# First-stage vectors through PSUM, leading products by kinds, and a fixed order of state-space banks in a two-block network on one core

## The chip, the cores and the metric

One core of a Trainium2 chip runs the whole kernel. TensorE multiplies, VectorE, ScalarE and GpSimd work on tiles, SP and ScalarE issue transfers. The metric is device time in microseconds from one launch; less is better. The kernel before took 1715.83 us in the median of three runs (1713.58 to 1717.22).

## The reference

A 512 x 1024 activation `x` goes through two blocks in fp32. Cut to what matters:

```python
x = layer_norm(x, ln_emb_g, ln_emb_b)                  # first stage
h = x @ w_in + b_in                                    # q, k, v, indexer, latents
mix = concat([swa_sink_attention(...), dsa_attention(...)]) @ w_o + b_o
x = layer_norm(ALPHA * x + mix, ln1_g, ln1_b)          # first norm
ca = memory_cross_attention(x, mem, ...)               # keys of mem are needed here
x = layer_norm(ALPHA * x + ca, ln2_g, ln2_b)           # second norm
f = square(relu(x @ w_up + b_up)) @ w_down + b_down
x = layer_norm(ALPHA * x + f, ln3_g, ln3_b)            # third norm
u = rms_norm(x, norm_w[0]); x = x + ssd_mixer(u, ...)  # state space: z, xbc, dt from u
u = rms_norm(x, norm_w[1]); x = x + mla_mixer(u, ...)  # fourth norm before it
return rms_norm(x, final_norm_w)
```

## The kernel before

Every fp32 operand of a product is split into a high and a low part, and a product is three: high by high, high by low, low by high (`mm3`, lines 129 to 131; which of 130 and 131 holds the low activations depends on which operand is stationary). `wload` (lines 115 to 125) brings a 512 KB weight into one of three raw buffers on SP's queue, ScalarE makes the high half (line 121), GpSimd the low half in two pieces (line 124); five split buffers follow. Activations are split by ScalarE (line 145) and VectorE (line 146) out of a PSUM bank of four transposes (`xpose`, line 279). The token axis has four tiles of 128 (`NT`).

The code is written as dataflow; a framework lays out each engine's instructions in one fixed order beforehand (`TileContext(..., schedule_with_timeline_sim=True)`) and inserts the waits. At run time every engine and queue keeps that order. PSUM has eight banks; `banks(...)` closes the pool of banks and opens one with other names (`acc`, `mm`, `px` and so on), and a bank that had another use before is waited for tile by tile.

First stage (`block1`): keys of the memory (`mem_k`, eight weights `xa_wk`, 24 products of 256 columns each) run while four tiles of `x` arrive. Each tile gets statistics (lines 326, 327), an inverse root (`nrstd`, lines 102 to 106: one ScalarE root, then four VectorE instructions of one column), gain and bias (lines 329, 330), its transposes, and later `ALPHA * r + b_o` (line 334), stored to `hd`. Gain, bias and `b_o` are rows of 1024 that are brought as 128 copies. Then `win_m` (96 products of 328 columns, accumulators `acc`), then `win_s`.

At every norm a helper `gemm_lead` (lines 170 to 182) computes the first four tiles of the next product while the last tokens are still being normalised: for token half 0 to 255, then 256 to 511, for each of four weights, for eight slices, one `mm3`. Between them `flush` issues the deferred transposes of the later tokens. It serves `xa_wq` (first norm), `w_up` (second), `ssm_xbc` (third) and `mla_z` (fourth). At the third norm `gate0` (line 1182) computes the gate products `z` of two token tiles ahead of it; the other two run in the state-space stage in banks `px`.

State-space stage (`block2a`): `conv` (lines 946 to 951) reads the four leading tiles in their banks, `ssm_dt` and `ssm_cum` make the decays, `prep` and `core` the chunks. Its banks are named `mm`, `px`, `py`, `po`.

Of the kernel before, what the change touches and what calls it, by code (L numbers as in the profile page):

```python
# [12 lines left out]
P = 128  # L13
# [11 lines left out]
class Net:  # L25
    def __init__(self, ctx, tc, a):
# [7 lines left out]
        self.banks(acc=4, mm=4)  # L34
# [28 lines left out]
    def mm(self):  # L63
        return self.bank("mm")
# [33 lines left out]
    def nrstd(self, pool, v, n, eps):  # L98
# [6 lines left out]
        nc.vector.scalar_tensor_tensor(y1, y0, v, y0, op0=ALU.mult, op1=ALU.mult)  # L105
        nc.vector.scalar_tensor_tensor(v, y1, -3.0, y0, op0=ALU.add, op1=ALU.mult)
# [63 lines left out]
    def gemm_lead(self, aps, X, tags):  # L170
        XH, XL = X
        W = [self.wload(ap) for ap in aps]
        pss = [self.bank(tag) for tag in tags]
        for lo in (0, 256):
# [115 lines left out]
    def block1(self, dbg):  # L290
# [21 lines left out]
        g = self.nbcast(lnp, "ln_emb_g", D, eng=nc.sync)  # L312
        b = self.bcast(lnp, "ln_emb_b", D, eng=nc.sync)
# [35 lines left out]
        snk = self.bcast(ap, "swa_sinks", 8)  # L349
        iw = ap.tile([P, NT, 8], F32, name="iw")  # L350
        bs = self.load(ap, "bin_s", [P, 13])
# [14 lines left out]
        rows = self.rows_load(self.mp)  # L366
        bm = self.bcast(ap, "bin_m", 328)
        kvg = self.bcast(ap, "dsa_kv_norm_g", P)
        ikg = self.bcast(ap, "idx_k_ln_g", 64)
        ikb = self.bcast(ap, "idx_k_ln_b", 64)  # L370
# [4 lines left out]
        for c, nk in enumerate((3, 3, 2)):  # L375
            wh, wl = self.wload(a["win_m"][:, c * 984:c * 984 + nk * 328], n=nk * 328)
            for kk in range(nk):
# [4 lines left out]
                k += 1  # L382
        cf = ap.tile([P, NT, P], F32, name="cf")
# [1258 lines left out]
```

## Time and profile before

| what | value |
|---|---|
| median of three runs | 1715.83 us (1713.58 to 1717.22) |
| profiled run | 1716.78 us |
| its span, first to last instruction | 1714.8 us |
| mean granted TensorE clock | 0.990 |
| TensorE busy | 1657.8 us, 97% |
| VectorE, ScalarE, GpSimd busy | 913.5, 835.6, 889.2 us |

The profile is of one execution. TensorE's busy time counts overlapping products once. In the rows, PE is TensorE, PEld its loads of the stationary operand, DVE VectorE, ACT ScalarE, POOL GpSimd, SP SyncE; `ACTq` and `SPq` are what an engine's sequencer issues. Idle time of an engine is put down to the instruction that released it.

### The profile page before, as it was taken

The numbers are of one execution on the slowest core, as the hardware profiler recorded it, in microseconds if no ns is written. First come the engines' busy times: TensorE is split into PE (matmuls) and PEld (weight loads), VectorE is DVE, ScalarE is ACT, GpSimd is POOL, SyncE is SP. The second block draws the span as 40 slices with busy tenths as digits, with TensorE's granted clock in tenths as the row PEclk, the third lists the DMA queues.
The fourth block names the chain that finished last, engine by engine and source line by source line (L and its number), as shares of the span: only waits on it lengthen the run. The fifth ranks groups of instructions, "written<-read, shape, count | busy, mean of one in ns | idle before, by whom it ended". The sixth has DMA issues, their size and how long they took to land.

```text
span 1714.8 us, 27158 instructions
## 1 busy us (share of the span) xinstructions
PE 1657.8 (97%) x10203; PEld 1477.9 (86%) x10203; DVE 913.5 (53%) x1965; ACT 835.6 (49%) x1694; POOL 889.2 (52%) x817
## 2 busy tenths in 40 slices
PE   6999999999999999999899999999999999999998
PEld 6877888889988888888878898889999888988998
DVE  7579763743663004402769877779221307667512
ACT  4455664453353124412558777776333426565532
POOL 6756433363374445543556777776544544344431
PEclk9999999999999999999999999999999999999999
DMA  8634313332232222222433333332434442123341
GB/s 286 201 104 130 105 50 114 127 111 78 96 111 98 86 98 93 92 98 78 145 107 99 99 110 100 105 112 86 148 110 136 137 132 66 54 69 97 107 142 50
DMA packets 68178, 187.20 MB, mean 109 GB/s; under 512 B 9968, under 2 KB 16544, under 8 KB 67792
## 3 DMA queue, kind: packets, MB, share of 16 engines
q1 hardware_dynamic: 50128, 152.95, 27.4%
q10 hardware_dynamic: 17632, 30.43, 5.6%
q8 instruction: 80, 1.31, 0.3%
q0 software_dynamic: 288, 2.10, 0.3%
q14 instruction: 50, 0.41, 0.1%
HBM read 163.86 MB, written 14.78 MB: 104 GB/s over the span
## 4 chain that ended last, share of the span: by engine, by line
PE 80%; DVE 10%; issue 3%; ACT 3%; DMA 2%; POOL 1%; ACTq 0%; DVEq 0%; SPq 0%; POOLq 0%
PE mm L129 15%; PE mm L131 15%; PE mm L130 15%; PE acc L130 5%; PE acc L131 5%; PE acc L129 5%; PE sc L130 2%; PE sc L131 2%; PE sc L129 2%; PE pv L130 1%; PE pv L131 1%; PE pv L129 1%; PE tr L887 1%; POOL wl L124 1%; DVE sc L479 1%
## 5 line engine op out<-in xcount | busy, mean ns | idle before, releaser
L124 POOL TENSOR_TENSOR wl<-wraw,wh 128x512 fp32r<-128x512 f32 (+1 forms) x498 | 658.0, 1346 | 509.7 <-ACT wh L121 477.4
L121 ACT ACTIVATE wh<-wraw 128x1024 fp32r<-128x1024 f32 (+4 forms) x254 | 258.5, 1019 | 409.6 <-PE acc L131 123.7
L129 PE MATMUL mm<-xaH,wh 128*128 128x512 f32 x552 | 221.2, 401 | 3.2 <-DVE qbL L140 1.3
L130 PE MATMUL mm<-xaL,wh 128*128 128x512 f32 x552 | 220.4, 399 | 0.0
L131 PE MATMUL mm<-xaH,wl 128*128 128x512 f32 x552 | 220.0, 399 | 0.0
L129 PE MATMUL mm<-wh,xaH 128*128 128x256 f32 x512 | 147.2, 288 | 1.4 <-ACT xaH L145 1.4
L130 PE MATMUL mm<-wl,xaH 128*128 128x256 f32 x512 | 145.6, 284 | 0.0
L131 PE MATMUL mm<-wh,xaL 128*128 128x256 f32 x512 | 145.2, 284 | 0.0
L129 PEld LDWEIGHTS mm<-xaH,wh 128*128 128x128 f32 x552 | 104.4, 189 | 27.2 <-DVE qbL L140 1.8
L131 PEld LDWEIGHTS mm<-xaH,wl 128*128 128x128 f32 x552 | 104.4, 189 | 23.7
L130 PEld LDWEIGHTS mm<-xaL,wh 128*128 128x128 f32 x552 | 104.5, 189 | 23.0
L878 POOL TENSOR_SCALAR S<-S,den 128x128 f32<-128x128 f32 (+1 forms) x96 | 50.9, 534 | 105.1 <-DVE den L877 89.0
L129 PEld LDWEIGHTS mm<-wh,xaH 128*128 128x128 f32 x512 | 97.8, 191 | 2.0 <-ACT xaH L145 1.8
L130 PEld LDWEIGHTS mm<-wl,xaH 128*128 128x128 f32 x512 | 97.7, 191 | 0.2
L131 PEld LDWEIGHTS mm<-wh,xaL 128*128 128x128 f32 x512 | 97.0, 190 | 0.1
L129 PE MATMUL mm<-wh,xbH 128*128 128x256 f32 x336 | 94.9, 283 | 0.7 <-DVE lnsum L256 0.5
L131 PE MATMUL mm<-wh,xbL 128*128 128x256 f32 x336 | 94.4, 284 | 0.1
L130 PE MATMUL mm<-wl,xbH 128*128 128x256 f32 x336 | 94.3, 282 | 0.0
L698 DVE TENSOR_TENSOR rl<-rl 128x512 f32<-128x512 f32 x32 | 43.7, 1366 | 78.4 <-ACT rl L697 78.4
L948 DVE SCALAR_TENSOR_TENSOR xbc<-mm,conv_w,xbc 128x511 f32<-128x511 f32 (+2 forms) x84 | 62.2, 741 | 11.6 <-ACT xbc L946 10.9
L876 ACT ACTIVATE S<-S,mx 128x128 f32<-128x128 f32 (+1 forms) x96 | 53.7, 560 | 24.2 <-DVE mx L875 22.1
L129 PEld LDWEIGHTS mm<-wh,xbH 128*128 128x128 f32 x336 | 63.6, 189 | 1.6 <-DVE lnsum L256 0.7
(633 smaller groups left out, 4747.4 us busy)
## 6 DMA issues: line engine op xcount, KB each, us to landing
wraw<-in_w_up SPq DMA_DIRECT2D x32, 512.0 KB, 3.3
wraw<-in_w_down SPq DMA_DIRECT2D x32, 512.0 KB, 3.2
wraw<-in_ssm_xbc SPq DMA_DIRECT2D x32, 512.0 KB, 3.3
Dm<-acd ACTq DMA_DIRECT2D x32, 256.0 KB, 3.2
wraw<-in_ssm_out SPq DMA_DIRECT2D x16, 512.0 KB, 3.5
wraw<-in_mla_z SPq DMA_DIRECT2D x16, 512.0 KB, 3.5
wraw<-in_mla_out SPq DMA_DIRECT2D x16, 512.0 KB, 3.6
wraw<-in_ssm_z SPq DMA_DIRECT2D x14, 512.0 KB, 3.3
```

Source lines behind the costliest of these rows:

```text
L121: nc.scalar.activation(h[:, :n], raw[:, :n], AF.Copy)
L124: (leng or nc.gpsimd).tensor_tensor(l[:, e], raw[:, e], f32(h[:, e]), op=ALU.subtract)
L129: mm(out, aH, bH, start=first, stop=False, skip_group_check=True)
L130: mm(out, aH, bL, start=False, stop=False, skip_group_check=True)
L131: mm(out, aL, bH, start=False, stop=last, skip_group_check=True)
L479: nc.vector.match_replace(out=scs[n], in_to_replace=m8, in_values=scs[n], imm_value=-3e38)
L698: nc.vector.tensor_tensor(r, r, r, op=ALU.mult)
L876: nc.scalar.activation(s, s, AF.Exp, bias=mx, scale=-1.0, accum_out=den)
L878: nc.gpsimd.tensor_scalar(s, s, den, 1.0, op0=ALU.mult, op1=ALU.mult)
L887: self.nc.tensor.transpose(pt[:, c], S[:, c], self.ident)
L948: nc.vector.scalar_tensor_tensor(o[:, j:], ps[:, :T - j], cw[:, m, 3 - j:4 - j], o[:, j:], op0=ALU.mult, op1=ALU.add)
```

## The change

Five edits. (1) Gain, bias and `b_o` come as one row each; each row is split, and TensorE spreads it over 128 partitions by a product with a row of ones (minus ones for the gain), into `gb` banks; lines 329, 330 and 334 work on halves and read PSUM. The pool of the first stage is `acc=2, mm=2, gb=4` and is reopened as `acc=4, mm=4` after the additions of `b_o`. (2) Small loads (`xa_bk`, `swa_sinks`, `bin_s`, `bin_m`, gains, the rows of biases) go from ScalarE's queue to SP's; the rows and `xa_bv` are issued after `win_m`. (3) Lines 105 and 106 take their second tensor as a column scalar. (4) `gemm_lead` and `gate0` run by kinds: high by high for all tiles, then low weights, then low activations. (5) The state-space pool takes its banks in the order `mm`, `po`, `px`, `py`.

```diff
-        self.banks(acc=4, mm=4)
+        self.banks(acc=2, mm=2, gb=4)
@@ nrstd
-        nc.vector.scalar_tensor_tensor(y1, y0, v, y0, op0=ALU.mult, op1=ALU.mult)
-        nc.vector.scalar_tensor_tensor(v, y1, -3.0, y0, op0=ALU.add, op1=ALU.mult)
+        nc.vector.tensor_scalar(y1, y0, v, y0, op0=ALU.mult, op1=ALU.mult)
+        nc.vector.tensor_scalar(v, y1, -3.0, y0, op0=ALU.add, op1=ALU.mult)
@@ gemm_lead
+        def kind(x, ts, q, last=False):
+            for i in ts:
+                for k in range(8):
+                    c = slice(k * P, (k + 1) * P)
+                    mm(pss[i][:, q], W[i][x == 2][:, c], (XH, XL)[x == 1][:, k, q], start=x == 0 and k == 0, stop=last and k == 7, skip_group_check=True)
         for lo in (0, 256):
             q = slice(lo, lo + 256)
-            for (wh, wl), ps in zip(W, pss):
-                for k in range(8):
-                    c = slice(k * P, (k + 1) * P)
-                    self.mm3(ps[:, q], wh[:, c], wl[:, c], XH[:, k, q], XL[:, k, q], k == 0, k == 7)
-                self.flush(n=1)
+            kind(0, range(4), q)
+            self.flush(n=1)
+            kind(2, (0, 1), q)
+            self.flush(n=1)
+            kind(1, (0, 1), q, True)
+            kind(1, (2, 3), q)
+            self.flush(n=1)
+            kind(2, (2, 3), q, True)
             self.flush()
@@ block1
-        g = self.nbcast(lnp, "ln_emb_g", D, eng=nc.sync)
-        b = self.bcast(lnp, "ln_emb_b", D, eng=nc.sync)
+        gb = lnp.tile([1, 3, D], F32, name="gb")
+        for i, key in enumerate(("ln_emb_g", "ln_emb_b", "b_o")):
+            nc.sync.dma_start(gb[:, i, :], a[key].unsqueeze(0))
+        self.kb = self.load(self.mp, "xa_bk", [P, 8], eng=nc.sync)
+        gbs = self.pair(lnp, [1, 3, D], "gbs")
+        def spread(i, v):
+            sg = lnp.tile([1, P], F32R, name=self.nm("sg"))
+            nc.scalar.activation(sg, self.mhalf[0:1, 0:1].to_broadcast([1, P]), AF.Copy, scale=-2.0 * v)
+            self.split(gbs[0][:, i, :], gbs[1][:, i, :], gb[:, i, :])
+            B = [self.bank("gb") for _ in range(2)]
+            for h in range(2):
+                for x in range(2):
+                    nc.tensor.matmul(B[h], sg, gbs[x][:, i, h * 512:h * 512 + 512], start=x == 0, stop=x == 1)
+            return B
+        GB = spread(0, -1.0) + spread(1, 1.0)
...
-        self.kb = self.load(self.mp, "xa_bk", [P, 8])
         self.mem_k(W, wk)
-        bo = self.bcast(lnp, "b_o", D, eng=nc.sync)
-        self.vb = self.bcast(self.mp, "xa_bv", D, eng=nc.sync)
...
-            nc.vector.scalar_tensor_tensor(r, r, mv[:, 0:1], g, op0=ALU.subtract, op1=ALU.mult)
-            nc.vector.scalar_tensor_tensor(r, r, mv[:, 1:2], b, op0=ALU.mult, op1=ALU.add)
+            for h in range(2):
+                rh = r[:, h * 512:h * 512 + 512]
+                nc.vector.scalar_tensor_tensor(rh, rh, mv[:, 0:1], GB[h], op0=ALU.subtract, op1=ALU.mult)
+                nc.vector.scalar_tensor_tensor(rh, rh, mv[:, 1:2], GB[2 + h], op0=ALU.mult, op1=ALU.add)
             self.xpose(r, xt, t)
+        B = spread(2, 1.0)
         for t in range(NT):
-            nc.vector.scalar_tensor_tensor(r, r, ALPHA, bo, op0=ALU.mult, op1=ALU.add)
+            for h in range(2):
+                rh = r[:, h * 512:h * 512 + 512]
+                nc.vector.scalar_tensor_tensor(rh, rh, ALPHA, B[h], op0=ALU.mult, op1=ALU.add)
             nc.sync.dma_start(self.hd[t], r)
         lp.close()
+        self.banks(acc=4, mm=4)
...
-        snk = self.bcast(ap, "swa_sinks", 8)
+        snk = self.bcast(ap, "swa_sinks", 8, eng=nc.sync)
...
-        rows = self.rows_load(self.mp)
-        bm = self.bcast(ap, "bin_m", 328)
+        bm = self.bcast(ap, "bin_m", 328, eng=nc.sync)
...
+        rows = self.rows_load(self.mp)
+        self.vb = self.bcast(self.mp, "xa_bv", D, eng=nc.sync)
@@ block1b
-        self.zpre = [self.gate0(self.bank("z"), W, t) for t in range(2)]
+        self.zpre = [self.bank("z") for _ in range(2)]
+        for kinds in ((0, 2), (1,)):
+            for t in range(2):
+                self.gate0(self.zpre[t], W, t, kinds)
@@ block2a
-        self.banks(mm=3, px=2, py=2, po=1)
+        self.banks(mm=3, po=1, px=2, py=2)
+        for tag, n in self.tags.items():
+            for _ in range(n):
+                self.bank(tag)
@@ gate0
+        for x in kinds:
+            for k in range(8):
+                n = slice((k % 3) * 288, (k % 3) * 288 + 288)
+                self.nc.tensor.matmul(ps[:, :288], u[x == 1][:, k, q], W[k // 3][x == 2][:, n], start=x == 0 and k == 0, stop=x == 1 and k == 7, skip_group_check=True)
```

## Rows read from the trace of the kernel before

**Rows 1.** Page, busy time, share of the span and instructions of each engine.

```profile
PE 1657.8 (97%) x10203; PEld 1477.9 (86%) x10203; DVE 913.5 (53%) x1965; ACT 835.6 (49%) x1694; POOL 889.2 (52%) x817
```

**Rows 2.** Waits of TensorE, whole span: waiter, releaser, total us, times, longest.

```profile
PE acc L129 <- ACT wh L121: 9.0, 3, 7.9
PE mm L279 <- DVE res L330: 4.7, 2, 4.4
PE sc L130 <- DVE xbL L146: 4.0, 1, 4.0
...
PE sc L130 <- DVE lnmu L264: 2.7, 1, 2.7
```

**Rows 3.** Waits of TensorE from 810 to 865 us.

```profile
PE px L129 <- DVE dts L1199: 2.8, 1, 2.8
PE z L131 <- DVE lnmu L265: 1.2, 1, 1.2
PE z L131 <- DVE lnmu L264: 1.0, 1, 1.0
PE z L131 <- DVE xaL L146: 0.8, 1, 0.8
```

**Rows 4.** Stretches: length, busy of PE, PEld, DVE, ACT, POOL, clock, DMA, GB/s.

```profile
0.00:15.80 15.80, 7.26 (x30) 6.58 (x31) 6.30 (x14) 6.37 (x8) 7.19 (x12) 1.00 0.88 308
15.80:32.70 16.90, 10.58 (x78) 9.33 (x77) 16.90 (x24) 5.95 (x10) 11.69 (x8) 1.00 0.86 327
32.70:48.20 15.50, 15.46 (x119) 15.46 (x119) 12.13 (x15) 8.32 (x13) 13.91 (x9) 0.89 0.63 188
48.20:62.90 14.70, 14.70 (x100) 14.70 (x98) 6.04 (x9) 6.57 (x10) 14.04 (x12) 1.00 0.84 260
839.08:852.70 13.62, 13.62 (x118) 13.62 (x117) 8.36 (x16) 9.20 (x15) 5.23 (x6) 1.00 0.29 87
```

**Rows 5.** Timeline of VectorE at the first norm: start, us, instruction, [idle before].

```profile
316.54 0.14 DVE L103 TENSOR_SCALAR lnvar<-lnvar 128x1 f32<-128x1 f32 x1
...
317.99 1.10 DVE L105 SCALAR_TENSOR_TENSOR nr<-nr,lnvar 128x1 f32<-128x1 f32 x1
...
319.08 2.29 DVE L576 SCALAR_TENSOR_TENSOR res<-res,xa_bo 128x1024 f32<-128x1024 f32 x1
321.30 1.21 DVE L106 SCALAR_TENSOR_TENSOR lnvar<-nr 128x1 f32<-128x1 f32 x1
...
322.50 1.27 DVE L146 TENSOR_TENSOR xbL<-tr,xbH 128x512 fp32r<-128x512 f32 x2
```

**Rows 6.** Groups of VectorE up to 63 us: busy, mean ns | idle before.

```profile
L334 DVE SCALAR_TENSOR_TENSOR res<-res,b_o 128x1024 f32<-128x1024 f32 x4 | 7.9, 1986 | 3.3 <-PE mm L279 3.3
L330 DVE SCALAR_TENSOR_TENSOR res<-res,mv,ln_emb_b 128x1024 f32<-128x1024 f32 x4 | 7.1, 1781 | 0.0
L329 DVE SCALAR_TENSOR_TENSOR res<-res,mv,ln_emb_g 128x1024 f32<-128x1024 f32 x4 | 6.1, 1529 | 0.0
L146 DVE TENSOR_TENSOR xaL<-mm,xaH 128x512 fp32r<-128x512 f32 x8 | 5.2, 677 | 0.0
...
L105 DVE SCALAR_TENSOR_TENSOR nr<-nr,mv 128x1 f32<-128x1 f32 x4 | 3.6, 912 | 0.0
```

**Rows 7.** Timeline of VectorE, last instruction of the first stage.

```profile
51.66 1.28 DVE L146 TENSOR_TENSOR xaL<-mm,xaH 128x512 fp32r<-128x512 f32 x2
```

**Rows 8.** Timeline of ScalarE and its queue, first stage and first norm.

```profile
12.52 1.06 ACT L121 ACTIVATE wh<-wraw 128x1024 fp32r<-128x1024 f32 x1 [3.10 <-DMA ng_dsa<-in_ng_dsa]
...
59.26 0.33 ACTq L71 DMA_DIRECT2D swa_sinks<-in_swa_sinks  x1
...
323.76 1.04 ACT L121 ACTIVATE wh<-wraw 128x1024 fp32r<-128x1024 f32 x1
```

**Rows 9.** Line 1078, all of its instructions: ns least, median, longest.

```profile
L1078 DVE TENSOR_SCALAR gss<-gss x16: 157/170/1462, 920.6 to 1215.1; 128x2 f32<-128x2 f32 x16
```

**Rows 10.** Page, issues of transfers: KB each, median us to landing.

```profile
wraw<-in_w_up SPq DMA_DIRECT2D x32, 512.0 KB, 3.3
```

More of the change, by code (lines that the diff above doesn't have):

```diff
@@ L173, in gemm_lead @@
         pss = [self.bank(tag) for tag in tags]
+        mm = self.nc.tensor.matmul
+        def kind(x, ts, q, last=False):
[3 more added lines that the diff above has]
+                    mm(pss[i][:, q], W[i][x == 2][:, c], (XH, XL)[x == 1][:, k, q], start=x == 0 and k == 0, stop=last and k == 7, skip_group_check=True)
         for lo in (0, 256):
             q = slice(lo, lo + 256)
-            for (wh, wl), ps in zip(W, pss):
-                for k in range(8):
-                    c = slice(k * P, (k + 1) * P)
-                    self.mm3(ps[:, q], wh[:, c], wl[:, c], XH[:, k, q], XL[:, k, q], k == 0, k == 7)
-                self.flush(n=1)
+            kind(0, range(4), q)
[6 more added lines that the diff above has]
+            kind(2, (2, 3), q, True)
             self.flush()
@@ L348, in block1 @@
         masks = {n: ap.tile([P, (n + 1) * P], F32R, name=f"mk{n}") for n in range(1, NT)}
-        snk = self.bcast(ap, "swa_sinks", 8)
+        snk = self.bcast(ap, "swa_sinks", 8, eng=nc.sync)
         iw = ap.tile([P, NT, 8], F32, name="iw")
-        bs = self.load(ap, "bin_s", [P, 13])
+        bs = self.load(ap, "bin_s", [P, 13], eng=nc.sync)
         c2 = ctx.enter_context(ExitStack())
@@ L365, in block1 @@
         ap = c3.enter_context(self.pool("small"))
-        rows = self.rows_load(self.mp)
-        bm = self.bcast(ap, "bin_m", 328)
-        kvg = self.bcast(ap, "dsa_kv_norm_g", P)
-        ikg = self.bcast(ap, "idx_k_ln_g", 64)
-        ikb = self.bcast(ap, "idx_k_ln_b", 64)
+        bm = self.bcast(ap, "bin_m", 328, eng=nc.sync)
+        kvg = self.bcast(ap, "dsa_kv_norm_g", P, eng=nc.sync)
+        ikg = self.bcast(ap, "idx_k_ln_g", 64, eng=nc.sync)
+        ikb = self.bcast(ap, "idx_k_ln_b", 64, eng=nc.sync)
         ms = [ap.tile([P, 328], F32, tag="ms", name=self.nm("ms"), bufs=4) for _ in range(NT)]
@@ L828, in rows_load @@
     def rows_load(self, ap):
-        return (self.load(ap, "bk_swa", [32, 384]), self.load(ap, "bk_dsa", [32, 640]), self.load(ap, "ng_swa", [8, 384]),
-                self.load(ap, "ng_dsa", [8, 640]), self.load(ap, "rel_bias", [32, 16]))
+        return [self.load(ap, k, s, eng=self.nc.sync) for k, s in (("bk_swa", [32, 384]), ("bk_dsa", [32, 640]), ("ng_swa", [8, 384]), ("ng_dsa", [8, 640]), ("rel_bias", [32, 16]))]
     def bias_tile(self, bt, ud, h, n, w):
@@ L1180, in gate0_w, with gate0 @@
         return [self.wload(self.a["ssm_z0"][:, c * 864:c * 864 + nk * 288], n=nk * 288) for c, nk in enumerate((3, 3, 2))]
-    def gate0(self, ps, W, t):
+    def gate0(self, ps, W, t, kinds=(0, 2, 1)):
         u = self.u
         q = slice(t * P, (t + 1) * P)
-        for k in range(8):
-            wh, wl = W[k // 3]
-            n = slice((k % 3) * 288, (k % 3) * 288 + 288)
-            self.mm3(ps[:, :288], u[0][:, k, q], u[1][:, k, q], wh[:, n], wl[:, n], k == 0, k == 7)
+        for x in kinds:
+            for k in range(8):
+                n = slice((k % 3) * 288, (k % 3) * 288 + 288)
+                self.nc.tensor.matmul(ps[:, :288], u[x == 1][:, k, q], W[k // 3][x == 2][:, n], start=x == 0 and k == 0, stop=x == 1 and k == 7, skip_group_check=True)
         return ps
```

## The prediction

> **What bounds the kernel now.** First the busy shares: TensorE is busy for 97% of the span, every other engine for about half [rows 1]. So whatever is removed from another engine counts only where TensorE stands still for it, and the next view is who TensorE waits for [rows 2]. The reader is to see how short that list is: 9.0 us on the first weights (7.9 of them before anything has arrived), 4.7 us in the first stage on VectorE (line 330) and 4.0 and 2.7 us at two norms on the low halves of the transposed activations (`xbL`, and a count that VectorE reaches late). One stretch, from the third norm on, adds 1.2, 1.0 and 0.8 us in the gate products `z` and 2.8 us at a state-space bank `px` [rows 3]. The change touches all of these but the first 7.9 us.
>
> Third, the stretches [rows 4]. Where nothing is missing, 118 products, nearly all 256 columns wide, fill 13.62 us, so one costs 0.12 us, one of 512 columns about 0.24. Up to 15.8 us 30 products keep TensorE busy for 7.26 us, 0.24 each: the start runs at half pace. From 15.8 to 32.7 it works 10.58 of 16.90 us, while VectorE is busy in all 16.90. From 32.7 to 48.2 it is full, but at a granted clock of 0.89.
>
> Fourth, why VectorE is late. At the first norm an instruction of one column takes 0.14 us at line 103, and 1.10 and 1.21 at lines 105 and 106 a moment later; these two read two tensors from SBUF, line 103 one, and GpSimd computes low halves of weights meanwhile. The additions with two SBUF tensors stretch likewise: line 576 took 2.29 us [rows 5], line 334 1.99 in the mean, while reading one operand from PSUM costs 0.677 us for 512 columns eight times over [rows 6]. VectorE instructions with two SBUF tensors wait for GpSimd; those with one do not, if they are one column wide.
>
> **The change part by part.** Terms are against the span of 1714.8 us; the profiled run took 1716.78, 0.95 above the median of 1715.83. I subtract them from the median.
>
> *First stage.* Removed are three broadcasts of 512 KB (gain, bias, `b_o`), and a fourth (`xa_bv`) moves behind `win_m`; 2.1 MB at 308 to 327 GB/s is 6.5 us of transfer out of a saturated beginning [rows 4]. That counts only where data was last, about 1.1 us of the 9.0. GpSimd's sign change goes too (off the path). VectorE now: lines 329, 330 and 334 took 6.1, 7.1 and 7.9 us [rows 6], 21.1 together. After: 24 halves with a PSUM operand at 0.677, 16.2. Line 105 took 3.6 for four, at 0.14 it is 0.6. Added are three splits of a 1024-column row, priced by the whole 1024-column split that two halves of 0.677 make: 1.35 each, 4.1. Net VectorE: -4.9 -3.0 +4.1 = -3.8, and line 106 saves some 2 more by the same reasoning. TensorE adds 12 products of 512 columns: eight while it runs at half pace (0.48) and four later (0.24), 4.8 us. ScalarE adds three splits and three short rows, in stretches where it works 6 of 16 us [rows 4].
>
> TensorE's sum: it would reach `win_m` at 48.2 - 4.7 (the wait for line 330) - 1.7 (15.5 us at 0.89 rather than near 1) - 1.1 (weights) + 4.8 = 45.5. There the new wait lies: `win_m`'s four accumulators are the first banks that the reopened pool hands out; if a pool hands out banks by the order of first use, as the code reads, these are the four `gb` banks. Two of them are read by VectorE to the last of the eight additions of `b_o`. VectorE ended its stage at 51.66 + 1.28 = 52.9 [rows 7]; less 5.8 that is 47.1, and the additions now come last. Behind the waiting product stand the other `win_m` products on TensorE, and then everything. Two of the four token tiles can start earlier (the bias halves are free after the last norm), so I count half of the 1.6 us: `win_m` begins at 46.3, and the stage gains **1.9 us**. Bounds: a gain of 6.0, if the broadcast products fall into idle time and no bank is late; a loss of 4.7, if VectorE still ends at 52.9 and all 14.7 us of `win_m` [rows 4] follow it (67.6 for 62.9).
>
> The small loads leave ScalarE's queue: its split of the second weight sat 3.10 us behind them [rows 8]. TensorE waited little there, so I count nothing. They now stand in SP's queue, past the weight loads; a weight load issues only when a raw buffer comes free, so small loads fit between, and a few tenths of issue each are hidden by three raw and five split buffers. Without that cover see the slow rival.
>
> *Four instructions of each norm.* Lines 105 and 106 become instructions with one tensor and two column scalars. No row shows this form. The nearest is line 103, 0.14 us beside a busy GpSimd [rows 5]; the far end is line 1078, two columns, 157 to 1462 ns [rows 9]. I take 0.14, as the width is the same. Elsewhere than in the first stage this only makes VectorE earlier at the norms, and is counted with them.
>
> The Trainium skill's "SBUF — State Buffer" (section "Who interferes with whom") speaks against this edit: an instruction with a scalar instead of a second tensor may enter a mode that takes both ports of VectorE, and then either engine blocks the other for a whole instruction. "VectorE: DVE Perf Modes" (section "Mode 2×_2P") ties that to an even count, or an odd one that is equal for source and destination; one column is the latter. Line 1078 behaves as the rule says, line 103 does not [rows 5, 9]; by the rule the edit would bring nothing, and rival 2 is how that would come out.
>
> *First norm's leading products* (`xa_wq`). TensorE stops for 4.0 us because products with `xbL` come early, and `xbL` is made at 322.50, behind lines 105, 576 and 106 [rows 2, 5]. By kinds, 32 products need only the high halves and 16 more only the low halves of weights: 48 x 0.12 = 5.8 us of work that covers the 4.0. But the fourth weight's high half starts only at 323.76 [rows 8], and the first kind wants all four. It stands behind ScalarE's square, which waits for VectorE; without 0.96 us at line 105 and 1.07 at 106 it comes at about 321.7 and is there at 322.8. TensorE's lead began near 318.6 (the 4.0 us end with the first half of `xbL` near 323.1, and four products ran ahead), so 24 products have ended at 321.5. I take 4.0 - 1.2 = **2.8 us** (1.0 to 4.0).
>
> *Second norm* (`w_up`): 2.7 us in the same place [rows 2]; its four weights are earlier, so **2.4 us** (1.0 to 2.7).
>
> *Third norm* (`z`, then `ssm_xbc`). Three waits on low halves, 1.2, 1.0 and 0.8 us, stand in the gate products [rows 3]. By kinds 32 gate products come before any with low activations. I take **2.6 us** of the 3.0 (1.0 to 4.0, the upper end if the second tile also comes 1.0 us earlier by line 105, as at the first norm). The fourth norm's lead has no row among the longer waits: **0.3 us** (0 to 0.8).
>
> The price of the kinds: of the four tiles of a lead the first is ready 32 products, 3.8 us, later than before, and two 1.9 us. They are read by ScalarE and VectorE while TensorE computes the next tiles in other banks; that covers it. If it does not, the next stage's first tile waits up to 3.8 us.
>
> *State-space banks.* `px` was first used, so it took the first two banks, which the leading products still held until the convolutions had read them: a gate tile waited 2.8 us [rows 3]. With the order of banks fixed, `px` gets the two that served the transposes of the norm, free long before. The wait is put down to line 1199, the addition of `dt`'s bias, which stands in VectorE's queue right behind the convolutions, and it reads another tile's bank; so I hold the bank to be the cause. Late next is the chain from the convolutions to the decays; the tiles that it starts from now end some 2 us later against TensorE. No row prices that; its bounds are nothing and the whole 2.8, and I take 0.8 of loss, near the lower one, because the same chain also starts from the gate tile, which comes earlier now: **2.0 us** (0 to 2.8).
>
> Sum: 1.9 + 2.8 + 2.4 + 2.6 + 0.3 + 2.0 = 12.0; 1715.83 - 12.0 = **1703.8 us**.
>
> **The rivals.**
> 1. *Everything lands at its good end*, because a freed VectorE also frees ScalarE's queue, where splits of weights stand behind roots and squares that wait for VectorE (the split at 323.76 is one) [rows 8]. First stage 6.0, norms 3.6 + 2.7 + 3.8 + 0.5, banks 2.8: 19.4, so 1696.4.
> 2. *The edited norm still waits for GpSimd*, as line 1078 does [rows 9]. Then line 105 keeps its 3.0 us in the first stage and 106 its 2, the additions of `b_o` end later and `win_m` with them: a loss of 1.5 for the gain of 1.9, and each of three norms loses about 0.8: 12.0 - 3.4 - 2.4 = 6.2, so 1709.6. For it: the row of two columns; against it: those of one.
> 3. *It doesn't do what it says*: TensorE waits for the fourth weight, or for late leading tiles, as long as it did for the low halves, and the decays eat the bank's gain: 1.0 + 1.0 + 1.0 + 0 and a stage at -1, so 2.0 and 1713.8, no measurable change.
> 4. *Slower: SP's queue is blocked.* The load of `swa_sinks` goes into memory that the first stage gives back late; on ScalarE's queue it was issued at 59.26 [rows 8]. If on SP it stands ahead of `win_m`'s first load and is issued as late, that load lands 3.3 us later (the median of such loads [rows 10]), its split takes 1.04 [rows 8], and `win_m`'s 14.7 us end at 78.3 for 62.9: 15.4 lost against 10.1 gained elsewhere, 1721.1. It decides once the block lasts past about 54 us. Against it: the load isn't ready when `win_m`'s are, and the order of a queue is laid out by readiness.
>
> **How the numbers follow.** The forecast has 0.47, rival 1 0.18, rival 2 0.18, rival 3 0.10, rival 4 0.07. About 0.2% (3.4 us) is what a measurement of this kernel can tell from no change: faster is below 1712.4, slower above 1719.3. Forecast, 1 and 2 are faster: 0.83; rival 3 the same: 0.10; rival 4 slower: 0.07. The bounds of the terms sum to 20.3 of gain and 1.7 of loss; the range leaves out rival 4, most of 3 and the far end of 1: 1694 to 1712.
>
> **What would show it.** Right: lines 105 and 106 near 0.14 us everywhere; no wait of TensorE on `xbL` or `lnmu` above 1 us at the norms; `px` with no wait before gate tile 3; the vector additions of the first stage near 0.68 us a half; `win_m` beginning near 46 us and ending near 61. Wrong: TensorE waiting at the first `acc` of `win_m` for VectorE; a wait for `wh` in the leads as long as the old one for low halves; the first broadcast product blocking TensorE before 15 us; SP idle on `swa_sinks` with weights behind it. The prediction fails most easily in the first stage, where order is laid out anew, and where a different order downstream opens waits that no row shows.

## The result, and the profile after

The changed kernel takes 1704.33 us in the median of four runs (1702.09 to 1705.58); the kernel before took 1716.53 us beside it (1713.58 to 1717.49). The ratio is 0.9926 with a 95% interval of 0.9913 to 0.9939, so it is faster by 0.6 to 0.9%. The forecast was 1703.8 us in a range of 1694 to 1712. The number came out; its terms did so only in part, and that two errors offset each other is luck. In two kernels one run of eleven took several milliseconds (`no_nr` 8096.69 us, `filler` 5511.26): the medians below include it, without it they are 1712.98 and 1714.38, and the ratios leave it out.

The profiled run took 1702.09 us, its span is 1700.3 us: 14.5 less than before, 2.3 more than the difference of the medians, because this run is the quickest of its four.

The page's line of busy time, to be read beside [rows 1]: TensorE is still the bound. It stands still for 47.0 us of its span in place of 57.0, and has 4.5 us less of busy time although it has 12 products more; the mean granted clock is 0.996 for 0.990.

```profile
PE 1653.3 (97%) x10215; PEld 1470.1 (86%) x10215; DVE 910.3 (54%) x1980; ACT 838.0 (49%) x1700; POOL 891.6 (52%) x816
```

TensorE's waits over the whole span (waiter, releaser, total us, times, longest), against [rows 2]: the first-stage wait for `res` and those for `xbL` and `lnmu` in the leads are gone, but a transpose waits 0.9 us for `xbL`. The wait of `px` ahead of a gate tile is gone too: the `px` row for line 1239 (line 1199 before) is another product, behind the gates at 847.89 us. In `z` 1.4 us for `xaH` are left, where it was 0.8 beside the three others. A longer wait has come, `py` for `X` in the state-space stage, 5.5 us where it was 3.0, and `px` for `xk` is new.

```profile
PE acc L129 <- ACT wh L121: 8.4, 2, 7.9
PE py L1084 <- DVE X L146: 5.5, 2, 3.2
...
PE px L1122 <- ACT xk L1040: 1.6, 1, 1.6
...
PE z L1228 <- ACT xaH L145: 1.4, 2, 1.1
...
PE po L130 <- DVE WL L146: 1.1, 2, 0.8
...
PE px L129 <- DVE dts L1239: 1.0, 1, 1.0
...
PE tr L292 <- DVE xbL L146: 0.9, 1, 0.9
```

Stretches of the first stage up to `win_m` (columns as in [rows 4]): from 15.8 to 32.7 us TensorE ends 118 products where it ended 78, and `win_m` begins at 44.57 us.

```profile
0.00:15.80 15.80, 7.60 (x40) 6.54 (x40) 8.20 (x15) 10.44 (x15) 5.11 (x7) 1.00 0.87 330
15.80:32.70 16.90, 15.95 (x118) 14.29 (x117) 16.11 (x36) 8.84 (x16) 12.47 (x9) 1.00 0.71 230
32.70:44.57 11.87, 10.80 (x82) 9.49 (x80) 9.73 (x17) 6.17 (x10) 10.59 (x10) 1.00 0.66 175
```

VectorE's groups up to 63 us, against [rows 6]: the 24 halves take 16.3 us (16.2 were forecast), the three splits of a row 5.5 (4.1 were forecast).

```profile
L357 DVE SCALAR_TENSOR_TENSOR res<-res,mv,gb 128x512 f32<-128x512 f32 x8 | 5.6, 743 | 0.0
L146 DVE TENSOR_TENSOR gbsL<-gb,gbsH 1x1024 fp32r<-1x1024 f32 x3 | 5.5, 1843 | 0.0
L356 DVE SCALAR_TENSOR_TENSOR res<-res,mv,gb 128x512 f32<-128x512 f32 x8 | 5.5, 734 | 0.0
...
L365 DVE SCALAR_TENSOR_TENSOR res<-res,gb 128x512 f32<-128x512 f32 x8 | 5.2, 683 | 1.7 <-PE mm L292 1.7
```

**Where the time went, by marks.** A mark is the start of a product that every variant has: the first of `win_m`, of the leads at the first and second norm, the first `z` at the third, the last gate product in `px`, the first of the `mla_z` lead. The lengths between marks, in us, from the profiled run of each kernel:

```
kernel       to win_m  to lead 1  to lead 2    to z   gates end  to mla_z   to end
before          48.18     270.28     129.81  367.59      47.68    419.02    432.20
after           44.57     271.43     125.29  364.51      39.37    422.68    432.47
no_nr           45.44     269.37     126.10  364.94      43.38    429.32    432.91
no_kinds        44.76     270.48     127.59  366.64      44.53    422.97    431.82
no_banks        44.93     269.55     125.22  364.51      44.20    425.00    431.40
nr_only         48.36     270.67     127.72  366.64      49.44    418.79    431.98
kinds_only      49.85     268.67     126.12  364.93      47.04    425.00    433.02
stage1_only     46.37     269.93     130.45  366.16      45.98    422.42    432.15
filler          49.23     266.65     128.87  368.23      45.99    422.15    432.12
xbc_tiles       44.04     267.41     125.20  364.56      39.48    430.23    432.88
loads_act       56.24     274.32     125.30  364.50      39.37    433.62    432.47
acd_late        43.88     269.37     125.24  364.56      39.16    425.06    431.60
dm_sp           45.05     270.13     125.24  364.65      39.24    423.10    431.49
gb_dm           50.89     269.93     125.29  364.51      39.37    424.44    431.73
```

From lead 1 to the end of the gates, kernels with both the kinds and the norm's edit repeat within 0.2 us where their code is the same. `before` and `stage1_only`, the same there too, differ by 0.6, 1.4 and 1.7, so a gain read against `before` alone is uncertain by about that. The granted clock goes with it. Both kernels wait 2.7 us at the second norm and 2.8 or 2.9 at `px`; behind these waits the clock is 0.64 and 0.53 in `before` (rows under `filler` below), and 1.00 twice in `stage1_only`:

```profile
450.20:454.00 3.80, 3.78 (x31) 3.78 (x32) 3.77 (x6) 1.54 (x3) 3.80 (x4) 1.00 0.48 174
855.78:859.43 3.65, 3.65 (x26) 3.60 (x27) 0.61 (x2) 2.38 (x3) 0.70 (x1) 1.00 0.34 129
```

The second column and the last but one scatter by several us even with the same code.

### The profile page after: what moved, and what is told of

It reads as the page before. It is cut to its first block, busy times and chain, and to the rows that moved or that the text cites. A ratio compares the mean times of both kernels' runs of the same rounds, so it can differ in the third digit from the quotient of the medians.

```text
span 1700.3 us, 27197 instructions
## 1 busy us (share of the span) xinstructions
PE 1653.3 (97%) x10215; PEld 1470.1 (86%) x10215; DVE 910.3 (54%) x1980; ACT 838.0 (49%) x1700; POOL 891.6 (52%) x816
## 4 chain that ended last, share of the span: by engine, by line
PE 78%; DVE 12%; ACT 3%; DMA 3%; issue 2%; POOL 1%; ACTq 0%; SPq 0%; DVEq 0%; POOLq 0%
PE mm L129 14%; PE mm L131 14%; PE mm L130 14%; PE acc L131 4%; PE acc L130 4%; PE acc L129 4%; PE sc L131 2%; PE sc L129 2%; PE sc L130 2%; PE tr L922 1%; DVE sc L512 1%; PE pv L130 1%; PE pv L131 1%; DVE xbc L983 1%; DVE m L511 1%
```

## The experiments

Names in the table are those of the kernels below. Each was timed beside the kernel before; ratios are to that, with their 95% interval.

**One part undone, the rest left.** `no_nr`:

```diff
-        nc.vector.tensor_scalar(y1, y0, v, y0, op0=ALU.mult, op1=ALU.mult)
-        nc.vector.tensor_scalar(v, y1, -3.0, y0, op0=ALU.add, op1=ALU.mult)
+        nc.vector.scalar_tensor_tensor(y1, y0, v, y0, op0=ALU.mult, op1=ALU.mult)
+        nc.vector.scalar_tensor_tensor(v, y1, -3.0, y0, op0=ALU.add, op1=ALU.mult)
```

> The changed kernel with lines 105 and 106 as they were (two tensors and a column). Theory: the kinds carry the norms, since 5.8 us of products cover a wait of 4.0; without the edit xbL and the fourth weight come 1 to 2 us later, which costs at most 1.2 us at each of three norms; in the first stage two instructions of about 1 us come back four times, and win_m begins about 2 us later (46.5 for 44.6). Together 2 to 5 us over the changed kernel: 1706 to 1709. Rival A: the edit carries the norms and kinds alone cover little: 8 us or more over it, above 1712. Rival B: the edit is worth nothing, as lines 105 and 106 wait for GpSimd in either form: no difference, 1704.3.

Measured 1713.27 us, 0.9984 (0.9975 to 0.9993): 9 us over the changed kernel. Rival A has the size, but its place is wrong. The first two norms lose 0.8 and 0.4 us, as the theory said. The gates lose 4.0 and the state-space stage 6.6. At the third norm VectorE's timeline shows the edit itself: first `no_nr`, then the changed kernel.

```profile
807.31 1.27 DVE L105 SCALAR_TENSOR_TENSOR nr<-nr,ss 128x1 f32<-128x1 f32 x1
808.51 1.30 DVE L105 SCALAR_TENSOR_TENSOR nr<-nr,lnvar 128x1 f32<-128x1 f32 x1
```

```profile
806.63 0.27 DVE L105 TENSOR_SCALAR nr<-nr,ss 128x1 f32<-128x1 f32 x1
806.81 0.27 DVE L105 TENSOR_SCALAR nr<-nr,lnvar 128x1 f32<-128x1 f32 x1
```

`no_kinds` puts `gemm_lead`, `gate0` and the call of the first two gate tiles back:

```diff
-            kind(0, range(4), q)
...
+            for (wh, wl), ps in zip(W, pss):
+                for k in range(8):
+                    self.mm3(ps[:, q], wh[:, c], wl[:, c], XH[:, k, q], XL[:, k, q], k == 0, k == 7)
```

> The changed kernel with the leading and gate products in their old order (line by line, three products for each part). Theory: beside the edit of the norm the kinds give 2.4 and 2.1 us at the first two norms (4.52 and 3.08 us of shift with both, 2.09 and 0.94 with the edit alone), and little at the third, where the convolutions begin no earlier; of that the state-space stage may give back about half: 2 to 5 us over the changed kernel, 1706 to 1709. Rival A: nothing is given back and the third norm counts too: 7 us over it, 1711. Rival B: VectorE and ScalarE set the beginning of the state-space stage whatever TensorE does: within 1 us, 1704.3 to 1705.

Measured 1710.64 us, 0.9965 (0.9951 to 0.9979): 6.3 over the changed kernel, near Rival A. The first two norms lose 2.3 and 2.1 us, as expected; the gates lose 5.2, where I had expected little, and the state-space stage gives nothing back. At the gates TensorE waits for low halves again:

```profile
PE z L131 <- DVE xaL L146: 2.9, 2, 2.5
```

`no_banks` takes the order of the state-space banks back (`banks(mm=3, px=2, py=2, po=1)`, and no loop that claims them).

> The changed kernel with the order of the state-space banks undone. Theory: the banks shorten the way to the end of the gate products by 4.6 us (13.77 us of lead over the kernel before at their begin, 18.4 at their end), but 4.0 of it is given back by 1164 us, since the chain of the convolutions and decays on ScalarE and VectorE does not come earlier; so here the gate products end some 4.6 us later, the waits of the changed kernel at 955.1 us (1.6, px for xk) and 959.3 us (2.3, py for X) shrink below 0.5 us, and the whole is 0.6 us over the changed kernel: 1705 us. Rival A: the gain of the banks lasts as I priced it: 2.0 us over the changed kernel, 1706.3. Rival B: it lasts in full and the 4.0 us are lost for another reason: 4.6 us over it, 1709, with the waits at 955 and 959 still there.

Measured 1707.43 us, 0.9961 (0.9948 to 0.9975): 3 us over the changed kernel by the medians, 6 by the ratios; either is more than the 0.6 of the theory. The gates lose 4.8. The wait of `px` is back, 3.2 us, and is put down to a convolution this time, which bears out that the bank was its cause:

```profile
PE px L1225 <- DVE xbc L986: 3.2, 1, 3.2
```

But the waits for `xk` (1.6) and `X` (2.3) stay as long as they were, so they are not what the banks' gain turned into. Of the theory the 4.6 us at the gates stand, and "given back by the same chain" falls.

**One part alone.** `kinds_only`, `nr_only` and `stage1_only` are the kernel before with one part of the change.

> The kernel before with the leading products and the gate products in the order of kinds, and nothing else. Theory: each wait of a norm costs twice, by its length and by the products at a granted clock of 0.53 to 0.66 in the 3.5 us behind it (about 1.6 us each), and the kinds remove both: 3.5, 3 and 3 us less what the fourth weight keeps (up to 1.2 at the first): 8.5 us under the kernel before, 1708. Rival A: only the waits count: 2.8, 2.4 and 2.6 less what the norm's edit had been worth, 6 us, 1710.5. Rival B: without the edit of the norm the fourth weight comes too late and the wait only changes its name: 1714 or more.

Measured 1715.82 us, 1.0002 (0.9991 to 1.0013): no change. The total is Rival B's, the way to it isn't. The kinds give 3.7 and 2.7 us at the first two norms, as expected, but at the gates only 0.6. TensorE's waits from 805 to 860 us show why: behind the low halves that came too early stand the transposes that VectorE's norm delays, and then the bank.

```profile
PE px L1204 <- DVE xbc L967: 3.2, 1, 3.2
PE z L1204 <- DVE lnmu L278: 1.7, 1, 1.7
PE mm L292 <- DVE un L758: 1.2, 1, 1.2
```

From the gates to `mla_z` 6.0 us are lost.

> The kernel before with lines 105 and 106 as instructions with two column scalars, and nothing else. Theory, from the marks of the runs so far: undoing the edit in the changed kernel cost 0.9 us in the first stage, 0.8 and 0.4 at the first two norms, 4.0 from the third norm to the end of the gate products and 6.6 in the first groups of the state-space stage, since VectorE is the engine that is late there. The last two terms do not need the kinds, so alone it gives about 8 us under the kernel before (and 2 more at the first two norms, where the low halves come earlier): 1707 to 1709. Rival: the edit pays only beside the kinds; alone the products with low halves still come too early and it gives 2 us or less: 1714.5.

Measured 1711.83 us, 0.9976 (0.9967 to 0.9985): 4.7 us under the kernel before, between theory and rival. In the profile the first norm gains 2.1, the second 0.9, the gates lose 1.8, since the order is laid anew and a transposed tile is now waited for (`z` for `xaH`), with the bank still behind it. This profiled run took 1715.55 us, the longest of its eleven, so it doesn't show where the 4.7 us of the median lie.

```profile
PE z L129 <- ACT xaH L145: 4.0, 2, 2.9
PE px L129 <- DVE dts L1199: 2.9, 1, 2.9
```

> The kernel before with the first stage of the changed one (vectors in PSUM, loads moved) and nothing else; lines 105 and 106 stay as they were. Theory: win_m begins at 45.4 as in the changed kernel without the norm's edit, 2.7 us earlier than before; some 1 us goes in win_m's own waits, so the kernel is 1.5 to 2 us under the kernel before: 1714.7. Rival A: the gain is lost before the first norm, where TensorE waits for VectorE and ScalarE at 200 to 220 us: 1716.5. Rival B: it is worth more than my 2 us since ScalarE's queue is free of small loads: 4 us, 1712.5.

Measured 1715.03 us, 0.9995 (0.9982 to 1.0008): 1.5 under the kernel before, near the 1714.7 of the theory but not told from no change. `win_m` begins at 46.37 where I expected 45.4.

**The price of a wait.** `filler` adds superfluous products ahead of two leads of the kernel before:

```diff
+        for r in range(4 if tags[0] == "sc" else 0):
+            for k in range(8):
+                self.nc.tensor.matmul(pss[0][:, :256], W[0][0][:, k * P:k * P + P], XH[:, k, :256], start=k == 0, stop=k == 7, skip_group_check=True)
```

> The kernel before with 32 superfluous products of 256 columns (3.84 us) ahead of the leading products of the first two norms; they need only high halves and their results are overwritten. Nothing else is moved, so the low halves come when they came. Theory: the 4.0 and 2.7 us of waiting are filled with work, the granted clock behind them stays near 1.00 in place of 0.57 and 0.66, and that gives back 1.6 us at each norm, less the 1.1 us by which the filling is longer than the second wait: 2 us under the kernel before, 1714.5. Rival: the slower products behind a wait have another cause than the wait (weights, banks): the filling adds 0 and 1.1 us, 1717.5, and the clock behind it is as low as before.

Measured 1715.16 us, 0.9993 (0.9983 to 1.0003), 1.5 us under the kernel before and not told from no change; the profile tells more than the time. Stretches behind the first norm's wait, in the kernel before (with the other two places there), then here:

```profile
323.20:327.00 3.80, 3.77 (x19) 3.77 (x20) 3.80 (x3) 1.79 (x4) 2.65 (x3) 0.57 0.42 138
451.70:455.50 3.80, 3.76 (x21) 3.76 (x22) 3.77 (x6) 1.54 (x3) 3.80 (x4) 0.64 0.51 195
858.85:862.50 3.65, 3.61 (x16) 3.64 (x17) 0.42 (x1) 1.44 (x2) 0.00 (x0) 0.53 0.33 125
```

```profile
322.20:326.00 3.80, 3.80 (x35) 3.80 (x34) 3.73 (x6) 1.35 (x4) 3.52 (x2) 1.00 0.43 142
```

The granted clock was 0.57 in the mean, so TensorE ran at 1.2 of its 2.4 GHz for most of the stretch, after it had stood still for 4.0 us; where it had worked through that time the clock was 1.00. The first norm's part is 0.94 us shorter (128.87 for 129.81) though it holds 3.84 us more of work and 0.7 of its 4.0 us of waiting: 3.84 - 3.3 would have made it 0.5 longer. So this wait cost 4.0 us and 1.5 more (2.1, read against `stage1_only`).

At the second norm the filling replaces 1.9 us of waiting (2.7 less the 0.5 and 0.4 that are left at transposes) and should cost 1.9. Against `before`, whose clock fell there to 0.64, the part is only 0.6 longer (368.23 for 367.59), so 1.3 came back; against `stage1_only`, whose clock stayed at 1.00 behind the same wait, it is 2.1 longer and nothing came back. So the theory holds where the clock falls, and it doesn't fall behind every such wait: behind the 2.7 us it fell in `before` alone of the four kernels that have them (`before`, `stage1_only`, `nr_only`, `no_kinds`), behind the 4.0 us in both that have them (`before`, `stage1_only`).

**The small loads.** `loads_act` puts `swa_sinks`, `bin_s`, `bin_m`, the three gains, the rows of biases and `xa_bv` of the changed kernel back on ScalarE's queue.

> The changed kernel with the small loads back on ScalarE's queue, where they stood before (the three rows and xa_bk stay on SP). Theory: on SP they sat ahead of the fifth weight (its buffer was free at 14.3 us, it was issued at 18.8) and TensorE waited 0.68 us for it; on ScalarE they sit ahead of splits instead, which cost a few tenths as well: within 1 us of the changed kernel, 1704.3. Rival A: holding the weight costs the whole 4 us behind it: 1700 to 1702 with the loads away from SP. Rival B: swa_sinks, whose memory is free late, now blocks splits of win_m on ScalarE: 1707.

Measured 1720.15 us (1712.06 to 1727.7), 1.0020 (1.0005 to 1.0036): some 16 us over the changed kernel; none of the three. Its ScalarE and VectorE at the start, and a stretch:

```profile
11.11 1.06 ACT L145 ACTIVATE mtH<-mraw 128x1024 fp32r<-128x1024 f32 x1 [3.35 <-DMA bk_swa<-in_bk_swa]
```

```profile
16.12 1.29 DVE L351 BATCH_NORM_STATS2 st<-res 128x6 f32<-128x512 f32 x2 [4.77 <-DMA res<-in_x]
```

```profile
15.80:32.70 16.90, 16.90 (x62) 13.40 (x61) 14.46 (x27) 5.23 (x8) 10.53 (x8) 1.00 0.69 257
```

The split of the memory waits behind the small loads, a tile of `x` comes late, and the half pace of the start lasts through the whole stretch: 62 products where the changed kernel ends 118. The pace changes at 33.2 us (12.1 in the changed kernel, 15.8 in the kernel before), although TensorE worked without a pause from 15.8 on; why so late isn't shown. `win_m` begins 11.7 us later. The granted clock reads 1.00 there, so that column doesn't show this half pace. This profiled run is the longest of the twelve, so its 11.7 us may be more than the loads cost in the median one.

**The state-space stage.** Three kernels try why the way from the gates to `mla_z` grew from 419.02 to 422.68 us. `xbc_tiles` computes the second half of the `ssm_xbc` lead tile by tile:

```diff
+            if tiles and lo:
+                for i in range(4):
+                    for k in range(8):
+                        c = slice(k * P, (k + 1) * P)
+                        self.mm3(pss[i][:, q], W[i][0][:, c], W[i][1][:, c], XH[:, k, q], XL[:, k, q], k == 0, k == 7)
+                    self.flush(n=1)
```

> The changed kernel, except that the second half of the ssm_xbc leading products goes tile by tile again (four tiles end one after another in place of all at the end). Theory: by kinds the first tile of the four is complete 3 to 4 us later, VectorE stands idle for 3.9 us ahead of the convolutions (836.07 us) while it is the late engine for the next 80 us; tile by tile the convolutions begin some 3 us earlier against the end of the leading products, the waits at 955.1 and 959.3 us shrink, and the kernel is 2 to 4 us under the changed one: 1701. Rival: the start of the convolutions is not what decides (ScalarE's copies, the gates or the weights are), or TensorE now waits for the low half of the last token tile: 1704.3 or up to 1 us more.

Measured 1707.32 us, 0.9946 (0.9934 to 0.9958): 3 us over the changed kernel, so the theory falls, and the rival's 1 us is too little. The convolutions do begin earlier, 28.2 us behind the first `z` for 30.3 (first the changed kernel's row, then this one's):

```profile
836.07 5.47 DVE L983 SCALAR_TENSOR_TENSOR xbc<-acc,conv_w,xbc 128x511 f32<-128x511 f32 x8 [3.88 <-ACT xbc L981]
```

```profile
829.43 4.94 DVE L989 SCALAR_TENSOR_TENSOR xbc<-acc,conv_w,xbc 128x511 f32<-128x511 f32 x7 [2.08 <-ACT xbc L987]
```

But TensorE waits more behind them. Its waits from 860 to 990 us, the changed kernel and then this one:

```profile
PE py L1084 <- DVE X L146: 2.3, 1, 2.3
PE px L1122 <- ACT xk L1040: 1.6, 1, 1.6
...
PE py L1085 <- DVE ML L146: 0.4, 1, 0.4
```

```profile
PE py L1090 <- DVE X L146: 2.3, 1, 2.3
PE po L129 <- DVE yo L1110: 1.7, 1, 1.7
PE px L1128 <- ACT xk L1046: 1.6, 1, 1.6
...
PE py L1091 <- DVE ML L146: 1.4, 2, 1.3
```

`loads_act` shows the same two extra waits (`yo` 1.7, `ML` 1.4) with the very order of instructions of the changed kernel from the first norm on. The first instruction there that falls behind by over 0.5 us, counted from `z`, is ScalarE's issue of `Dm` loads: it waits for the write of `acd` 3.0 us in place of 2.4, and 0.94 us at that point are 7.7 at the `py` of 960.67 us. `acd_late` is built to make that delay:

```diff
+            for _ in range(4):
+                nc.vector.tensor_scalar_mul(at, at, 1.0)
             nc.sync.dma_start(acd, at)
```

> The changed kernel with four superfluous multiplications by one (128 columns each, 0.2 to 0.3 us) on VectorE ahead of the write of acd. It makes the write, and with it the loads in ScalarE's queue, about 1 us later. In the kernel with its small loads on ScalarE's queue the write landed 0.94 us later (by the same order of instructions) and that shift had grown to 7 to 8 us by the waits at 955 to 960 us. Theory: the stage enlarges the delay, since every wait that it opens is followed by products at a lower granted clock: 5 to 8 us over the changed kernel, 1710 to 1712. Rival: the delay goes through as it is, 1 us, 1705.3, and that kernel's 8 us have another cause.

Measured 1702.01 us, 0.9920 (0.9906 to 0.9933): not slower at all. The order was laid anew, the third convolution went ahead of the loads on ScalarE, and the write was issued 5.4 us later, counted from `z`. That is not the delay alone, so it neither shows nor refutes that the stage enlarges one.

`dm_sp` takes the loads off ScalarE's queue:

```diff
-            nc.scalar.dma_start(Dm, acd[...])
+            (nc.sync if g == 0 and c < 3 else nc.scalar).dma_start(Dm, acd[...])
```

> The changed kernel, except that the first three decay loads (Dm from acd, line 1059) are issued on SP's queue in place of ScalarE's. In the changed kernel ScalarE's queue stands still from 873.3 to 876.2 us: the load waits there 2.4 us for the write of acd to land, and three loads take 0.45 us each to issue, while a convolution waits behind them. Theory: this is where the state-space stage takes back what the norms gave; with the loads on SP ScalarE goes on with the convolution some 2.5 us earlier, VectorE's and TensorE's waits of 879 to 881 us (1.1 and 1.0) and of 955 to 959 us (1.6 and 2.3) shrink, and the kernel is 2 to 4 us under the changed one: 1701. Rival A: VectorE's convolutions are the bound with or without it: 1704.3. Rival B: SP's queue now holds weights back for 2.4 us, and TensorE waits for one: 1706.

Measured 1698.68 us (1698.18 to 1700.92), 0.9902 (0.9887 to 0.9916): the fastest of all, 5.6 us under the changed kernel by the medians, 4 by the ratios, whose intervals just overlap. ScalarE's timeline, the changed kernel and then this one (the first row is its queue):

```profile
874.81 1.30 ACTq L1059 DMA_DIRECT2D Dm<-acd  x3
876.21 0.60 ACT L985 ACTIVATE mm<-xbc 128x512 f32<-128x512 f32 x1 [2.91 <-DVE xbc L983]
```

```profile
874.56 0.60 ACT L985 ACTIVATE mm<-xbc 128x512 f32<-128x512 f32 x1 [2.04 <-DVE xbc L983]
```

From `z` that convolution comes 0.9 us earlier, not 2.5, since VectorE is late next. The waits for `xk` and `X` at 955 to 959 us are gone, which is what the theory wanted, but others have come: from the gates to `mla_z` it takes 423.10 us for 422.68, and the two profiles differ by only 1.4 us in all. That the loads' queue costs something is likely by the medians; the place and the size aren't shown.

**The rows without their low part.** `gb_dm` is `dm_sp` with the three rows as they are, in f32, and no split:

```diff
+                nc.tensor.matmul(B[h], sg, gb[:, i, h * 512:h * 512 + 512], start=True, stop=True)
```

> The kernel with the decay loads on SP, and in the first stage the three rows go as they are (f32, one product of 512 columns for each half, a row of plus or minus one as weights) in place of a high and a low part. That takes three additions of 1x1024 from VectorE (2.20, 1.16 and 2.17 us in the changed kernel, 5.5 together, where I had counted 4.1) and three splits from ScalarE; TensorE has 6 products for 12. No row has such an f32 product; transposes of f32 take 0.13 us for 128 columns, so an estimate is 0.5 us each, and up to twice that. Theory: VectorE is the late engine of the first stage, the first norm comes earlier by the 3.4 us of the first two splits, win_m begins 2 to 3 us before 45.05 us, and the whole is 2 to 3 us under the kernel with the decay loads on SP (1698.7): 1696. Rival A: the first norm waits for the loads of x or for the weights and win_m begins where it did: 1698.7. Rival B: f32 products are so slow that TensorE loses what VectorE gains: 1699 to 1701.

Measured 1707.09 us, 0.9950 (0.9934 to 0.9966): 8.4 over `dm_sp`, Rival B and more. TensorE at the start:

```profile
11.31 7.19 PE L335 MATMUL gb<-gb,sg 1*128 1x512 f32 x8
18.43 0.58 PE L130 MATMUL acc<-mtL,wh 128*128 128x256 f32 x1
```

The four f32 products are eight records of 0.9 us, 1.8 for a product, but at the half pace of the start, which lasts to 22.4 us here. The changed kernel's split ones run behind its start and take 0.73 for two; like is compared with like by the later f32 products of this kernel, 1.12 each:

```profile
28.40 1.12 PE L335 MATMUL gb<-gb,sg 1*128 1x512 f32 x2
```

VectorE got what was promised (its first half-tile of the norm at 13.45 us in place of 21.43), but then waits for transposes behind TensorE, 7.8 us at one of them. In this stage TensorE's work counts as much as VectorE's; how much of the 8.4 us is the f32 product and how much the longer half pace isn't shown.

## Why the prediction was right, point by point

The sum, in the profiled pair: to the first norm 1.9 forecast, 2.5 measured; first norm 2.8 and 4.5; second 2.4 and 3.1; third norm with the gates 2.6 + 2.0 and 8.3; the state-space stage behind them -3.7 (0.8 of loss was counted within the 2.0); fourth norm to the end 0.3 and -0.3. Together 12.0 and 14.4. The medians give 12.2. The norms and the gates gave 15.9 for 9.8, and what was too little there the state-space stage took back: that the total came out within 0.2 us is luck. The largest thing left out is the clock. At a mean of 0.990 over 1714.8 us some 17 us are lost to the lower clock, at 0.996 over 1700.3 some 7: 10 of the 14.5 us, part of it while TensorE stood still. The forecast counts 1.7 of them, in the first stage.

- **First stage.** The size was right, its parts were not: `win_m` began at 44.57 us for 46.3 and lasted until 60.92 (before: 62.9), so 1.7 longer than the 14.7 of before. The halves took what was forecast, and at the feared bank TensorE waited 0.2 us. Mis-sized were the splits of a row (2.20, 1.16 and 2.17 us for 1.35 each; the two long ones ran beside GpSimd's splits, the short one began while GpSimd was idle) and the columns (0.25 and 0.20 for 0.14). The step that failed is the small loads, "so I count nothing": with them on ScalarE (`loads_act`) the kernel is 16 us slower, and in the profiled run 11.7 of its 25.5 us stand ahead of `win_m`. A small form of the fourth rival is there too: on SP ten of them stand ahead of a weight, which is issued at 18.79 us; but `swa_sinks` came behind `win_m`'s loads (54.82 us) and blocked nothing. One of the ten is `xa_bv`: it stands behind `win_m` in the code, but was issued at 18.25 us (before: 18.05), so that its 512 KB did not leave the beginning, as the prediction had it.

```profile
18.25 0.42 SPq L71 DMA_DIRECT2D xa_bv<-in_xa_bv  x1
18.79 0.35 SPq L120 DMA_DIRECT2D wraw<-in_xa_wk  x1
```

- **Lines 105 and 106.** Right: 0.19 to 0.28 us in all 56 instructions, with GpSimd busy or idle, so the second rival falls. By the rule that the Trainium skill gives in "SBUF — State Buffer" (section "Who interferes with whom") and "VectorE: DVE Perf Modes" (section "Mode 2×_2P") this form could have been blocked by GpSimd; the trace shows no such block, with these 0.19 to 0.28. What the Trainium skill's page on the modes asks for is an outermost non-unit dimension that is even, or odd and equal for both; that a single column counts as one was my reading, not the page's words. What I had wrong is its weight: undone, it costs 9 us, of which the forecast's way of counting (with the norms) holds 1.2.
- **First and second norm.** The mechanism was right, the term was too small. I took waits at their length, 4.0 and 2.7. Behind the first the products ran at a granted clock of 0.57, worth 1.5 us (`filler`); I had counted the clock in the first stage only. 4.0 + 1.5 less a wait of 0.9 that is left (a transpose, at 328.74) is 4.6, and 4.5 was measured. The fourth weight, for which I took 1.2 off, is in no wait of the two leads.
- **Third norm and banks.** 8.3 us for 4.6. The waits of 3.0 and 2.8 went, and the slow products behind `px` (16 in 3.65 us; 48 such take 6.54 in the changed kernel, so 1.5 us): 7.3 of the 8.3. The 1.5 belong to this run of the kernel before; `stage1_only` has the wait without them, and its gates are 1.7 us shorter. My adding up was wrong in kind: undoing the norm's edit, the kinds or the banks costs 4.0, 5.2 and 4.8 us there, the kinds alone give 0.6, the norm's edit alone loses 1.8. Each removes one wait of a row of them, and the next one takes its place until all are gone.
- **State-space stage.** "I take 0.8 of loss, near the lower one" was too little, 3.7 in the profiled pair. That the chain from convolutions to decays is late next is right as far as TensorE waits there for `X`, `xk`, `WH` and `WL`; that it comes from the banks has `no_banks` against it: there the waits stay and the stretch is 2.3 us longer still.
- **First rival** (all at its good end, 1696.4): the norms and the gates did go there and beyond (15.9 us for 12.9); the state-space stage (-3.7) and the first stage (2.5 for 6.0) kept the total from it. **Third rival**: it needed TensorE to wait in the leads for a weight, and it doesn't.

**Open:** what sets the length from the gates to `mla_z`. It went from 418.8 to 433.6 us over these kernels, and by 10.9 between the changed kernel and `loads_act` with the same order of instructions. No single cause was shown for it, and the part of the 12.2 us that belongs there is known only to several us. What it consists of can be read: that stretch in `before`, the changed kernel and `loads_act`, all with the same products.

```profile
863.54:1282.56 419.02, 411.28 (x2785) 377.69 (x2783) 294.31 (x479) 276.29 (x597) 276.92 (x236) 0.99 0.33 106
845.17:1267.85 422.68, 411.09 (x2784) 376.43 (x2783) 304.57 (x484) 278.56 (x601) 284.01 (x238) 0.99 0.34 107
859.73:1293.35 433.62, 418.03 (x2785) 382.01 (x2783) 307.24 (x484) 278.61 (x601) 282.89 (x238) 0.98 0.31 104
```

TensorE stands still for 7.7, 11.6 and 15.6 us. So the 3.7 us that the changed kernel loses are waiting; of the 10.9 of `loads_act` 4.0 are waiting and 6.9 slower products, at a clock of 0.98.

## What to carry to other kernels

Price a wait of TensorE as its length plus what the products behind it may lose at a lower granted clock, here 1.5 us on a wait of 4.0; behind waits of 2.7 and 2.8 us it was lost in one run and not in another, so look at the clock in more than one. Where several waits stand in a row in one stretch, neither doing one repair alone nor undoing one gives its share: do both before crediting a part. A load that waits for another transfer is worth moving out of the queue of an engine that has late work behind it, though its price wasn't shown here; and small loads are free only as long as nothing behind them in their queue is needed first.

## What the runs showed of the hardware that was not expected

- VectorE's one-column instruction with two column scalars took 0.19 to 0.28 us, with GpSimd busy or idle; with two tensors 1.27 and 1.30 at the third norm of `no_nr`.
- An addition of a single row of 1024 from two SBUF inputs took 2.20 and 2.17 us beside GpSimd's splits and 1.16 when it began with GpSimd idle: one partition wide, it is stretched like those of 128.
- An f32 product of a 512-column row shows as two records and took 1.12 us (1.8 at the half pace of the start), against 0.36 for one of a split row.
- A write of 64 KB to DRAM delayed the loads that read it by 2.4 us on another engine's queue, 3.0 in another run.
